# Low part of every second half weight block: ScalarE and an accumulating GpSimd DMA in place of a VectorE subtraction

## The chip, the core and the metric

The kernel runs on one core of a Trainium2 chip. The metric is device time in microseconds from launch to end, the median of several executions. The engines named here are TensorE (PE in the profile, PEld for its weight loads), VectorE (DVE), ScalarE (ACT), GpSimd (POOL) and SyncE (SP, which only issues DMAs).

## What is computed

The reference is a two-layer trunk over 256 latent tokens and 256 context tokens of width 2048. Each layer projects all tokens with a 2048 x 8192 weight matrix, runs a gated short convolution on one half of the features and an eight-head bidirectional retention on the other, and projects back with a 2048 x 2048 matrix.

```python
shift, scale, gate = split(silu(c) @ w_mod + b_mod, 3)
hx = rmsnorm(x, norm_w) * (1 + scale) + shift
a_h, a_b, a_c, a_z, q, k, v, r_z = split(hx @ w_in)
y_conv = silu(a_z) * rmsnorm(a_b * short_conv(a_c * a_h, conv_w), conv_norm_w)
y_ret  = silu(r_z) * headnorm(retention(rope(q), rope(k), v, states of the context))
x = x + gate * (concat(y_conv, y_ret) @ w_out)
```

The context goes through the same layer in layer 0. In layer 1 only its keys and values are needed, since the output holds the 256 latent tokens alone. After the second layer there is a last RMSNorm.

## The kernel before

**Precision.** All large products are made of float32 numbers split in two parts of TensorE's reduced type (fp32r): a high part, which is the rounded number, and a low part, which is the number minus its high part. `split` (L368) makes both: ScalarE writes the high part (L369), VectorE subtracts (L370). `mm3` (L343) then adds three products: high by high, high by low, low by high. Where only the 256 latent tokens are needed, `mmx` (L350) has the same three products in two matmuls per block, one of 512 columns (L353) for the high weights and one of 256 columns (L354) for the low weights.

**Weights.** Weights come in *pieces* of 128 x 1024 float32 numbers (512 KB, eight blocks of 128 x 128), in the order in which TensorE uses them. SyncE loads a piece into one of `RAW` = 6 buffers named `raw`. There are 512 pieces: 256 of `w_in` (`wi`), 64 of `w_out` (`wo`), 64 (`wm`) and 128 (`wd`) of the modulation matrix. Only the first two kinds are split, by *half pieces* of 128 x 512 numbers (four blocks), into the tiles `whi` and `wlo`. Both have `WH` = 4 buffers, so a half piece takes the buffers that the half piece four places before it has left. `pump` (L287) issues loads and splits in program order as buffers come free; it is called after each half piece that TensorE has been given (`block_done`, L335), so every engine's order is fixed when the program is written.

```python
WH, AHEAD = 4, 3
if self.wsplit - self.wused >= self.WH or s > self.at + self.AHEAD: break
self.split(self.raw[s][:, 512 * hf:512 * hf + 512], hi, lo)
```

A `raw` buffer is given to a new load once the instructions that read its second half have ended.

**Order.** `build_program` (L197) lists the steps. Per layer: first the seven tiles of `P` (all rows of weights, seven output tiles at once), then one tile of 128 output features after the other (`F`: conv tiles A_*, then per head K, Q and R_Z), with two steps `V` for the values, then `OG` and `O` for the output projection. In layer 1 the K tiles and V run over 512 tokens (`mm3`); conv tiles, Q, R_Z and the output projection run over 256 (`mmx`). Steps `D` between them are rows of the modulation matrix, which VectorE multiplies and sums (L535). A `P`, `F` or `O` tile of 16 blocks uses two pieces, that is four half pieces.

In layer 1, pieces over 256 tokens are 64 for the conv tiles (with `P`), 16 for Q, 16 for R_Z and 32 for the output projection.

Of the kernel before, what the change touches and what calls it, by code (L numbers as in the profile page):

```python
# [13 lines left out]
AF = mybir.ActivationFunctionType  # L14
ALU = mybir.AluOpType
# [5 lines left out]
NX = 256  # L21
# [3 lines left out]
EPS = 1e-6  # L25
# [140 lines left out]
class Trunk:  # L166
# [25 lines left out]
    def bank(self, kind, name="b"):  # L192
        return self.psum.tile([P, NT], F32, tag=kind, name=name)

# [1 line left out]

    def build_program(self):  # L197
        prog = []
# [88 lines left out]
    def pump(self):  # L287
        nc = self.nc
        while True:
            did = False  # L290
            while self.nload < len(self.seq) and (self.nload < self.RAW or self.free[self.nload - self.RAW]):
                kind, i = self.seq[self.nload]
                t = self.praw.tile([P, 1024], F32, tag="raw", name="raw")
                nc.sync.dma_start(t, self.io[kind][i])
                self.raw[self.nload] = t
                self.nload += 1
                did = True
            while self.nsplit < 2 * self.nload:
                s, hf = divmod(self.nsplit, 2)
                if self.weight(s):  # L300
                    if self.wsplit - self.wused >= self.WH or s > self.at + self.AHEAD:
                        break
                    hi = self.pw.tile([P, 512], F32R, tag="whi", name="whi")
                    lo = self.pw.tile([P, 512], F32R, tag="wlo", name="wlo")
                    self.split(self.raw[s][:, 512 * hf:512 * hf + 512], hi, lo)
                    self.parts[s, hf] = (hi, lo)
                    self.wsplit += 1
                    if hf == 1:
                        self.free[s] = True
                        del self.raw[s]  # L310
                elif s > self.at + self.AHEAD:
                    break
                self.nsplit += 1
                did = True
            if not did:
                return
# [21 lines left out]
            del self.parts[s, b // 4]  # L338
            self.pump()

# [1 line left out]

    def mm3(self, out, w, h, first, last):  # L343
        (whi, wlo), (hhi, hlo) = w, h
# [3 lines left out]
        mm(out, lhsT=wlo, rhs=hhi, start=False, stop=last)  # L348

    def mmx(self, out, w, t, first, last):  # L350
        """As mm3, for the NX tokens of t alone; the two halves of out have to be added."""
        mm = self.nc.tensor.matmul
        mm(out.rearrange("p (s t) -> p s t", s=2), lhsT=w[0], rhs=t[:, :, :NX], start=first, stop=False)  # L353
        mm(out[:, :NX], lhsT=w[1], rhs=t[:, 0, :NX], start=False, stop=last)  # L354
# [7 lines left out]
    def mm(self, out, w, t, n, first, last):  # L362
        if n == NX:
            self.mmx(out, w, t, first, last)
        else:
            self.mm3(out, w, (t[:, 0, :], t[:, 1, :]), first, last)

    def split(self, src, hi, lo):  # L368
        self.nc.scalar.activation(hi, src, AF.Copy)  # L369
        self.nc.vector.tensor_tensor(lo, src, hi.bitcast(F32), op=ALU.subtract)  # L370

    def smv(self, name):
        lo, hi = SM[name]
        return self.sm[:, lo:hi]
# [52 lines left out]
        nc.vector.tensor_scalar(self.lg[:, 64:96], e, -256.0, None, op0=ALU.mult)  # L427

    def rsqrt(self, ps, n, dim, out):
        """out = -2 * dim / sqrt(ps / dim + EPS)"""  # L430
        nc = self.nc
        r, t = self.tmp("rr")[:, :n], self.tmp("rt")[:, :n]
        nc.scalar.activation(r, ps, AF.Abs_reciprocal_sqrt, scale=1.0 / dim, bias=self.eps)
        nc.scalar.activation(t, r, AF.Square)
        nc.vector.scalar_tensor_tensor(t, ps, dim * EPS, t, op0=ALU.add, op1=ALU.mult)
        nc.vector.scalar_tensor_tensor(out, t, -3.0 * dim, r, op0=ALU.add, op1=ALU.mult)
# [43 lines left out]
        self.nc.tensor.matmul(ps, lhsT=self.ones, rhs=src, start=True, stop=True)  # L480
        self.rsqrt(ps, n, dim, out)

# [1 line left out]

    def mod_step(self, idx):
        nc = self.nc
# [64 lines left out]
            self.h[k] = self.pair("h")  # L551
        self.split(xn, self.h[k][:, 0, cols], self.h[k][:, 1, cols])

# [1 line left out]

    def n_tok(self, l, f):
        return NT if l == 0 or K <= f < R_Z else NX
# [75 lines left out]
        self.split(src, y[:, 0, :], y[:, 1, :])  # L633
        self.y[k] = y

# [1 line left out]

    def conv_post(self, l, j, pc, ph, pb, pz):
        nc = self.nc
# [30 lines left out]
        nc.vector.scalar_tensor_tensor(sz[:, :n], sz[:, :n], 1.0, pz[:, :n], op0=ALU.add, op1=ALU.mult)  # L670
        return sz

# [1 line left out]

    def rope(self, ps, n):
        nc = self.nc
# [30 lines left out]
        return t1, t2  # L707

    def attend(self, l, h, st):
        """The steps of one head's retention, each with work for TensorE."""  # L710
        nc = self.nc
        n = NT if l == 0 else NX
        q, k, v = st["q"], st["k"], st["v"]
        t1, t2 = st["mask"]
        msl = [slice(P, P + NX), slice(0, NX)]
        e = slice(P * (h % 4), P * (h % 4) + P)
        fin = lambda out, ps, m: nc.vector.scalar_tensor_tensor(out, ps, K_SCALE, m, op0=ALU.mult, op1=ALU.mult)
        tiles = {}

        def parts(name, w):  # L720
            s = self.tmp(name)[:, :w]
            hi, lo = self.tmp(name + "h", dt=F32R)[:, :w], self.tmp(name + "l", dt=F32R)[:, :w]
            return s, hi, lo

        def score(out, c, qc):
            self.mm3(out, (k[0][:, c], k[1][:, c]), (q[0][:, qc], q[1][:, qc]), True, True)

        def ctx_scores(t):
            ps = self.bank("att", "sc")[:, :n]
            score(ps, slice(NX + P * t, NX + P * t + P), slice(0, n))  # L730
            s, hi, lo = parts("sc", n)
            fin(s[:, :NX], ps[:, :NX], t2[:, msl[t]])
            if l == 0:
                fin(s[:, NX:], ps[:, NX:], t1[:, msl[t]])
            self.split(s, hi, lo)
            tiles[t] = (hi, lo)

        def x_scores():
            ps = self.bank("att", "sx")
            s, hi, lo = parts("sx", NT)  # L740
            for t in range(2):
                c = slice(NX * t, NX * t + NX)
                score(ps[:, c], slice(P * t, P * t + P), slice(0, NX))
                fin(s[:, c], ps[:, c], t1[:, msl[t]])
            self.split(s, hi, lo)
            tiles[2] = (hi, lo)

        def weigh(t):
            if t == 0:
                st["po"] = self.bank("att", "po")  # L750
            po = st["po"]
            hi, lo = tiles[t]
            if t < 2:
                self.mm3(po[:, :n], (v[0][:, 2 + t, e], v[1][:, 2 + t, e]), (hi, lo), t == 0, False)
                return
            for i in range(2):
                c = slice(NX * i, NX * i + NX)
                self.mm3(po[:, :NX], (v[0][:, i, e], v[1][:, i, e]), (hi[:, c], lo[:, c]), False, i == 1)
            sq = self.tmp("osq")[:, :n]
            nc.scalar.activation(sq, po[:, :n], AF.Square)  # L760
            hi, lo = self.tmp("osh", dt=F32R)[:, :n], self.tmp("osl", dt=F32R)[:, :n]
            self.split(sq, hi, lo)
            st["sq"] = (hi, lo)

        def finish():
            ps = self.bank("att", "st")[:, :n]
            for i in range(2):
                nc.tensor.matmul(ps, lhsT=self.onesr, rhs=st["sq"][i], start=(i == 0), stop=(i == 1))
            r = self.tmp("hr")[:, :n]
            self.rsqrt(ps, n, P, r)  # L770
            g = self.slot("yf") if l == 0 else self.tmp("yg")
            nc.vector.scalar_tensor_tensor(g[:, :n], st["po"][:, :n], self.smc("gn", l * 8 + h), r,
                                           op0=ALU.mult, op1=ALU.mult)
            nc.vector.tensor_tensor(g[:, :n], g[:, :n], st["sz"][:, :n], op=ALU.mult)
            self.yf[8 + h] = g
            if l == 1:
                self.y_prep(l, 8 + h)

        def run(*fns):
            return lambda: [f() for f in fns]  # L780

        return [run(lambda: ctx_scores(0), lambda: ctx_scores(1)), run(lambda: weigh(0), x_scores),
                lambda: weigh(1), lambda: weigh(2), finish]

# [1 line left out]

    def load_res(self, l, f):
        if f >= KT:
# [29 lines left out]
        elif segs[0] == 0:  # L818
            nc.scalar.dma_start(self.scratch[f], o[:, :NX])

# [1 line left out]

    def run(self):
        nc = self.nc
# [171 lines left out]
```

## Time and profile before

| | before |
|---|---|
| time, median of 2 runs | 1576.28 us (1575.01 to 1577.54) |
| span of the profiled execution | 1574.7 us |
| TensorE busy | 1537.8 us, 98% |
| VectorE busy | 1153.4 us, 73% |
| ScalarE busy | 701.5 us, 45% |
| GpSimd busy | 0.7 us, 0% |
| mean granted TensorE clock | 0.995 of full speed |
| bytes moved by DMAs | 287.24 MB, mean 182 GB/s |

The span runs from the first to the last instruction of one profiled execution. The times of the two runs are 0.3 and 2.8 us above it. A matmul that the profile shows as 0.40 us long overlaps the next; what a matmul costs is the distance from one start to the next.

### The profile page before, as it was taken

What the parts mean: (1) busy time and instruction counts of PE and PEld (TensorE: products, weight loads), DVE (VectorE), ACT (ScalarE), POOL (GpSimd) and SP (SyncE); (2) the same over time, 40 slices, a digit from 0 to 9 for tenths busy, and PEclk for the clock granted to TensorE, in tenths of its full rate; (3) what the DMA queues carried; (4) which work ended last, traced back from release to release, by engine and by line L of the source; (5) the groups of instructions that cost most, each with busy time, mean ns of one, the idle gap of its engine ahead of it and who ended that gap; (6) DMA issues with size and microseconds to landing.
All of it is one profiled execution on the core that took longest, in us unless ns stands there. A gap on an engine that the chain in (4) does not pass through costs nothing.

```text
span 1574.7 us, 20880 instructions
## 1 busy us (share of the span) xinstructions
PE 1537.8 (98%) x7486; PEld 1249.8 (79%) x7486; DVE 1153.4 (73%) x2236; ACT 701.5 (45%) x1243; POOL 0.7 (0%) x6
## 2 busy tenths in 40 slices
PE   4999999999999999999999999999999999999996
PEld 2556888888888888888888888888888888888885
DVE  4345997777767666776678887889886877677775
ACT  4223432222224444344545332566553565466663
POOL 0000000000000000000000000000000000000000
PEclk9999999999999999999999999999999999999998
DMA  8989575555653233433335776556786444443563
GB/s 316 341 294 328 181 223 190 184 181 192 195 172 121 94 114 105 158 119 99 116 95 176 248 229 211 154 183 216 264 284 201 133 126 139 164 148 108 174 217 104
DMA packets 84631, 287.24 MB, mean 182 GB/s; under 512 B 9392, under 2 KB 13616, under 8 KB 84400
## 3 DMA queue, kind: packets, MB, share of 16 engines
q1 hardware_dynamic: 81648, 282.77, 54.9%
q10 hardware_dynamic: 2880, 3.15, 0.6%
q8 instruction: 58, 0.95, 0.2%
q14 instruction: 45, 0.37, 0.1%
HBM read 281.69 MB, written 4.19 MB: 182 GB/s over the span
## 4 chain that ended last, share of the span: by engine, by line
PE 95%; DVE 2%; ACT 1%; DMA 1%; issue 0%; SPq 0%; DVEq 0%; ACTq 0%
PE acc L346 16%; PE acc L348 16%; PE acc L347 16%; PE acc L353 12%; PE acc L354 6%; PE vps L348 4%; PE vps L347 4%; PE vps L346 4%; PE mod L496 2%; PE p L346 2%; PE p L347 2%; PE p L353 2%; PE p L348 2%; PE ops L353 1%; PE ops L346 1%; PE ops L347 1%
## 5 line engine op out<-in xcount | busy, mean ns | idle before, releaser
L369 ACT ACTIVATE whi<-raw 128x512 fp32r<-128x512 f32 x640 | 402.1, 631 | 662.4 <-PE acc L347 353.7
L370 DVE TENSOR_TENSOR wlo<-raw,whi 128x512 fp32r<-128x512 f32 x640 | 437.4, 688 | 235.8 <-ACT whi L369 220.2
L346 PE MATMUL acc<-h,whi 128*128 128x512 f32 x912 | 355.7, 390 | 1.6 <-DVE vc L603 1.6
L348 PE MATMUL acc<-h,wlo 128*128 128x512 f32 x912 | 355.3, 390 | 0.0
L347 PE MATMUL acc<-h,whi 128*128 128x512 f32 x912 | 355.2, 389 | 0.0
L353 PE MATMUL acc<-h,whi 128*128 128x512 f32 x656 | 232.7, 398 | 0.0
L346 PEld LDWEIGHTS acc<-h,whi 128*128 128x128 f32 x912 | 171.2, 188 | 37.2 <-ACT whi L369 2.4
L348 PEld LDWEIGHTS acc<-h,wlo 128*128 128x128 f32 x912 | 171.2, 188 | 35.8
L347 PEld LDWEIGHTS acc<-h,whi 128*128 128x128 f32 x912 | 171.2, 188 | 34.7
L354 PE MATMUL acc<-h,wlo 128*128 128x256 f32 x656 | 184.3, 281 | 0.0
L353 PEld LDWEIGHTS acc<-h,whi 128*128 128x128 f32 x656 | 123.2, 188 | 29.7
L535 DVE CUSTOM_DVE_ANT_0 junk<-raw,cb,sm 128x1024 bf16<-128x1024 f32 x112 | 142.1, 1278 | 0.1
L535 DVE CUSTOM_DVE_ANT_0 junk<-raw,cb,mvp 128x1024 bf16<-128x1024 f32 x112 | 141.8, 1278 | 0.1
L354 PEld LDWEIGHTS acc<-h,wlo 128*128 128x128 f32 x656 | 123.9, 189 | 0.2
L346 PE MATMUL vps<-whi,h 128*128 128x512 f32 x256 | 100.4, 392 | 0.0
L348 PE MATMUL vps<-whi,h 128*128 128x512 f32 x256 | 99.8, 390 | 0.0
L347 PE MATMUL vps<-wlo,h 128*128 128x512 f32 x256 | 99.7, 390 | 0.0
L347 PE MATMUL acc<-y,whi 128*128 128x512 f32 (+1 forms) x208 | 77.7, 374 | 0.0
L348 PE MATMUL acc<-y,wlo 128*128 128x512 f32 (+1 forms) x208 | 77.5, 373 | 0.0
L346 PE MATMUL acc<-y,whi 128*128 128x512 f32 (+1 forms) x208 | 77.5, 373 | 0.0
L353 PE MATMUL acc<-y,whi 128*128 128x512 f32 x192 | 67.9, 399 | 0.0
L346 PEld LDWEIGHTS vps<-whi,h 128*128 128x128 f32 x256 | 48.1, 188 | 10.1 <-issue 0.2
(194 smaller groups left out, 1977.7 us busy)
## 6 DMA issues: line engine op xcount, KB each, us to landing
raw<-wi SPq DMA_DIRECT2D x256, 512.0 KB, 3.8
raw<-wd SPq DMA_DIRECT2D x128, 512.0 KB, 4.3
raw<-wm SPq DMA_DIRECT2D x64, 512.0 KB, 6.0
raw<-wo SPq DMA_DIRECT2D x64, 512.0 KB, 3.7
xs<-xc SPq DMA_DIRECT2D x16, 256.0 KB, 5.4
xr<-xc SPq DMA_DIRECT2D x16, 256.0 KB, 5.5
cb<-cb SPq DMA_DIRECT2D x1, 2048.0 KB, 11.1
scratch<-x ACTq DMA_DIRECT2D x16, 128.0 KB, 3.7
```

What stands on the lines that cost most here:

```text
L346: mm(out, lhsT=whi, rhs=hhi, start=first, stop=False)
L347: mm(out, lhsT=whi, rhs=hlo, start=False, stop=False)
L348: mm(out, lhsT=wlo, rhs=hhi, start=False, stop=last)
L353: mm(out.rearrange("p (s t) -> p s t", s=2), lhsT=w[0], rhs=t[:, :, :NX], start=first, stop=False)
L354: mm(out[:, :NX], lhsT=w[1], rhs=t[:, 0, :NX], start=False, stop=last)
L369: self.nc.scalar.activation(hi, src, AF.Copy)
L370: self.nc.vector.tensor_tensor(lo, src, hi.bitcast(F32), op=ALU.subtract)
L496: nc.tensor.matmul(self.modps[32 * j:32 * j + 32, :n], lhsT=self.csp[:, k, :], rhs=raws[o // 1024][:, o % 1024:o % 1024 + n], start=(i == ...
L535: nc.vector.tensor_tensor_reduce(junk, raw, self.cb[:, D * m + 1024 * hf:D * m + 1024 * hf + 1024], 1.0, init, ALU.mult, ALU.add, out[:, f ...
```

## The change

In the pieces from number 256 on, the low part of the second half piece is no longer made by VectorE. ScalarE writes the high part as before, then writes the negated raw block into `wlo` (it is rounded to fp32r there in the same way as the high part), and GpSimd issues a DMA that adds the raw block to `wlo` in place. 198 of the 256 last pieces are weights that are split; all others of the 640 half pieces keep the old way. Piece 256 is the first of the last K tile of layer 0, so the change covers that head's three tiles, layer 0's output projection and all of layer 1.

```diff
+                    src = self.raw[s][:, 512 * hf:512 * hf + 512]
+                    if hf == 1 and s >= 256:
+                        self.split_dma(src, hi, lo)
+                    else:
+                        self.split(src, hi, lo)
-                    self.split(self.raw[s][:, 512 * hf:512 * hf + 512], hi, lo)
...
+    def split_dma(self, src, hi, lo):
+        nc = self.nc
+        nc.scalar.activation(hi, src, AF.Copy)
+        nc.scalar.activation(lo, src, AF.Copy, scale=-1.0)
+        nc.gpsimd.dma_start(lo, src, accum_op=ALU.add)
```

The rows below are the program's order of one engine, with the source line, the operation, and output and input tiles with their buffer names. First ScalarE before, in layer 1's output projection, around one output tile (two pieces, four half pieces):

```order
L369 ACTIVATE whi_14249<-raw_14084 128x512
L455 ACTIVATE sq_14234<-x2_14231 128x256
L817 ACTIVATE x2_14231<-x2_14231,sm_84 128x256
L369 ACTIVATE whi_14261<-raw_14084 128x512
L369 ACTIVATE whi_14273<-raw_14110 128x512
L369 ACTIVATE whi_14285<-raw_14110 128x512
```

ScalarE after, at the same place; `sq` and `x2` belong to the previous output tile:

```order
L466 ACTIVATE sq_14428<-x2_14425 128x256
L373 ACTIVATE whi_14443<-raw_14273 128x512
L828 ACTIVATE x2_14425<-x2_14425,sm_84 128x256
L379 ACTIVATE whi_14455<-raw_14273 128x512
L380 ACTIVATE wlo_14456<-raw_14273 128x512
L373 ACTIVATE whi_14468<-raw_14300 128x512
L379 ACTIVATE whi_14480<-raw_14300 128x512
L380 ACTIVATE wlo_14481<-raw_14300 128x512
```

One more instruction stands behind the high part of each second half piece. VectorE before, at the same place:

```order
L808 SCALAR_TENSOR_TENSOR x2_14231<-acc_14182,mv1_141,xr_14057 128x256
L370 TENSOR_TENSOR wlo_14228<-raw_14049,whi_14227 128x512
L811 SCALAR_TENSOR_TENSOR x2_14231<-acc_14182,mv1_141,x2_14231 128x256
L370 TENSOR_TENSOR wlo_14250<-raw_14084,whi_14249 128x512
L456 TENSOR_TENSOR ssq_13660<-ssq_13660,sq_14234 128x256
L370 TENSOR_TENSOR wlo_14262<-raw_14084,whi_14261 128x512
L370 TENSOR_TENSOR wlo_14274<-raw_14110,whi_14273 128x512
```

VectorE after:

```order
L819 SCALAR_TENSOR_TENSOR x2_14425<-acc_14374,mv1_141,xr_14245 128x256
L822 SCALAR_TENSOR_TENSOR x2_14425<-acc_14374,mv1_141,x2_14425 128x256
L467 TENSOR_TENSOR ssq_13836<-ssq_13836,sq_14428 128x256
L374 TENSOR_TENSOR wlo_14444<-raw_14273,whi_14443 128x512
L374 TENSOR_TENSOR wlo_14469<-raw_14300,whi_14468 128x512
```

Every second subtraction is gone from VectorE. Each of them is a DMA on GpSimd's queue now, which had none before:

```order
L381 DMA wlo_14396<-raw_14210 128x512
L381 DMA wlo_14421<-raw_14237 128x512
L381 DMA wlo_14456<-raw_14273 128x512
L381 DMA wlo_14481<-raw_14300 128x512
L381 DMA wlo_14513<-raw_14337 128x512
```

These are five of the 198; nothing else stands between them on that queue.

## Rows read from the trace of the kernel before

**Rows 1.** Page, part 1: busy us, share of the span, instructions.

```profile
span 1574.7 us, 20880 instructions
...
PE 1537.8 (98%) x7486; PEld 1249.8 (79%) x7486; DVE 1153.4 (73%) x2236; ACT 701.5 (45%) x1243; POOL 0.7 (0%) x6
```

**Rows 2.** Page, part 4: share of the ending chain by engine.

```profile
PE 95%; DVE 2%; ACT 1%; DMA 1%; issue 0%; SPq 0%; DVEq 0%; ACTq 0%
```

**Rows 3.** Busy time by stretch (us from the span's start).

```profile
core 0: us, PE busy (x) PEld busy (x) DVE busy (x) ACT busy (x) POOL busy (x), PEclk, DMA share, GB/s
20.00:40.00 20.00, 16.67 (x108) 8.42 (x108) 7.85 (x22) 4.50 (x8) 0.00 (x0) 0.83 0.81 309
970.00:1180.00 210.00, 209.87 (x1197) 182.69 (x1196) 177.54 (x380) 119.92 (x236) 0.00 (x0) 1.00 0.67 218
1100.00:1165.00 65.00, 65.00 (x371) 56.33 (x370) 54.82 (x106) 35.19 (x67) 0.00 (x0) 1.00 0.82 274
1180.00:1450.00 270.00, 269.00 (x1352) 225.38 (x1351) 200.23 (x414) 146.96 (x275) 0.00 (x0) 1.00 0.46 147
1450.00:1555.00 105.00, 104.97 (x600) 90.83 (x599) 77.33 (x149) 66.36 (x124) 0.00 (x0) 1.00 0.54 171
```

**Rows 4.** Page, part 5: the two halves of the weight split.

```profile
L369 ACT ACTIVATE whi<-raw 128x512 fp32r<-128x512 f32 x640 | 402.1, 631 | 662.4 <-PE acc L347 353.7
L370 DVE TENSOR_TENSOR wlo<-raw,whi 128x512 fp32r<-128x512 f32 x640 | 437.4, 688 | 235.8 <-ACT whi L369 220.2
```

**Rows 5.** ScalarE's groups by line, 970 to 1165 us.

```profile
L369 ACT ACTIVATE whi<-raw 128x512 fp32r<-128x512 f32 x129 | 81.3, 632 | 70.9 <-PE acc L353 42.0 <-PE p L353 11.2 <-PE acc L347 10.4
```

**Rows 6.** Timeline of ScalarE, layer 1's output projection: start us, us.

```profile
1497.69 0.63 ACT L369 ACTIVATE whi<-raw 128x512 fp32r<-128x512 f32 x1
1498.23 0.49 ACT L817 ACTIVATE x<-x,sm 128x256 f32<-128x256 f32 x1
1499.10 0.63 ACT L369 ACTIVATE whi<-raw 128x512 fp32r<-128x512 f32 x1 [0.38 <-PE acc L353]
```

**Rows 7.** Timeline of TensorE over the same weights.

```profile
1498.90 0.28 PE L354 MATMUL acc<-y,wlo 128*128 128x256 f32 x1
...
1502.08 0.28 PE L354 MATMUL acc<-y,wlo 128*128 128x256 f32 x1
...
1503.49 0.28 PE L354 MATMUL acc<-y,wlo 128*128 128x256 f32 x1
```

**Rows 8.** DMA view, whole span: KB each, median us to landing.

```profile
xr<-xc SPq DMA_DIRECT2D x16, 256.0 KB, 5.5
...
out<-fo SPq DMA_DIRECT2D x4, 256.0 KB, 2.3
```

**Rows 9.** DMA view, 970 to 1165 us.

```profile
q1 hardware_dynamic: 11168, 40.66, 64.7%
...
raw<-wi SPq DMA_DIRECT2D x62, 512.0 KB, 4.2
raw<-wd SPq DMA_DIRECT2D x16, 512.0 KB, 4.4
scratch<-x ACTq DMA_DIRECT2D x3, 128.0 KB, 1.7
```

**Rows 10.** View of the tile raw, same stretch, its last row.

```profile
DMA to landing us min/median/max: 3.3/4.3/7.5
```

**Rows 11.** Tile xr: its issue on SyncE's queue, ns min/median/max.

```profile
L792 SPq DMA_DIRECT2D xr<-xc x16: 383/424/433, 841.9 to 958.2; - x16
```

**Rows 12.** Timeline of TensorE near the start: idle time in brackets.

```profile
27.80 0.80 PE L346 MATMUL p<-h,whi 128*128 128x512 f32 x1 [1.31 <-ACT whi L369]
28.39 0.63 PE L347 MATMUL p<-h,whi 128*128 128x512 f32 x1
28.82 0.63 PE L346 MATMUL p<-h,whi 128*128 128x512 f32 x1
```

## The prediction

> **What bounds the kernel now.** I read the page's busy times and its chain first: TensorE is busy for 98% of the span and carries 95% of the chain that ended last [rows 1, 2]. VectorE, from which the change takes work, carries 2%. So VectorE is not what the time waits for as a whole. Then the busy times by stretch, for layer 1, which holds most of the changed half pieces: from 970 to 1555 us TensorE is busy for 209.87 + 269.00 + 104.97 = 583.84 of 585 us [rows 3]. All that a faster VectorE could give back there is 1.2 us, although VectorE itself is nearly as full (177.54 of 210 us in the conv tiles). What matters is therefore whether each low part is still there in time.
>
> How early it is made is read from the timelines of ScalarE and TensorE in layer 1's output projection. The high part of one second half piece starts at 1499.10 us, when TensorE gives up the buffer: its last matmul with the old low part starts at 1498.90 and lasts 0.28 [rows 6, 7]. TensorE reads the new low part first at 1503.49. So **4.39 us** lie between. That is no accident of this place: four buffers leave three half pieces of work for TensorE between a buffer's release and its next use, and one half piece over 256 tokens takes 1503.49 - 1502.08 = 1.41 us [rows 7]. In the conv stretch the grouped waits say the same: most of what ScalarE waits for ahead of a high part is TensorE, 42.0 of 70.9 us from one line alone [rows 5]; it starts as soon as a buffer is released and not before. The old way needs 0.63 us for the high part and 0.69 us for the subtraction [rows 4], 1.3 us of the 4.39.
>
> **The change part by part.** *Removed:* 198 subtractions of 688 ns [rows 4], 136 us of VectorE. By the first paragraph this is worth 0 to 1.2 us; I take 1.
>
> *Added on ScalarE:* 198 copies at 631 ns [rows 4], 125 us. In the conv tiles 64 of them bring ScalarE from 119.92 to 160 of 210 us, in the output projection 32 bring it from 66.36 to 87 of 105 [rows 3]: more, but with room. The new copy waits for TensorE's last use of the old low part; that ended at 1499.18, before the copy can start. What is queued behind it (the next high part, then `sq` and the scaling of `x2`) moves by one copy, about 0.6 us, and those high parts have some 3 us to spare. Nothing here.
>
> *Added in the chain of each changed low part:* copies follow each other by 0.54 us (1497.69 to 1498.23) and last 0.63 [rows 6], so the negated block is ready 1.17 us after the high part starts. Then comes X, the time from there until GpSimd's DMA has landed. TensorE waits if 1.17 + X is over 4.39, that is **if X is over 3.2 us**. It waits at the first matmul that reads the low part and everything behind it in its order waits too. The chain restarts at the release four half pieces earlier, and within it lies one other changed half piece, whose stall counts for both; so each changed half piece costs half of the excess, (1.17 + X - 4.39) / 2.
>
> *How many pay:* of layer 1's pieces over 256 tokens, 64 for the conv tiles, 16 for R_Z and 32 for the output projection, 112 in all with the short window. The 16 of Q have a K tile (twice the work) or a head's own matmuls ahead of them; I put 4 us for them all, an estimate. K, V and layer 0 run over 512 tokens, where three half pieces are about twice 4.2 us; they pay only if X is over some 7 us.
>
> *What X is.* No row shows a DMA that GpSimd issues or one that adds. Bounds from other DMAs: below, 2.3 us for a 256 KB store in the quiet end of the kernel [rows 8], and even 1.7 us for 128 KB in the conv stretch [rows 9]; above, 7.5 us, the slowest landing of a raw piece in that stretch [rows 10]. Nothing lands in less than the lower ones, so a negative cost has no ground beyond VectorE's 1 us. Between them, an adding DMA has to read its source and its destination, 512 KB for a 256 KB block, and it does so beside the weight loads, whose own queue already fills 64.7% of the 16 engines [rows 9] and 82% with all traffic in 1100 to 1165 us [rows 3]. The nearest row by bytes and by load is thus the raw piece, 512 KB in 4.2 to 4.4 us [rows 9, 10]. The 256 KB load in 2 KB rows, the same shape as the block, took 5.5 us [rows 8]. The issue itself took 0.42 us for such a shape on SyncE's queue [rows 11], and GpSimd has to issue too, so I add it in full: X = 4.3 + 0.4 = **4.7 us**.
>
> The Trainium skill prices this lower. In DMA: Bandwidth & Descriptors, section "Anatomy of one DMA — SWDGE (gpsimd) path", a DMA issued by GpSimd costs about 2.0 us plus its bytes over 436 GB/s. For 256 KB that is an estimate of 2.6 us, under the point of 3.2, and by it the change would cost nothing. By the same fit the raw pieces would land after 3.2 us: the trace's fastest in the conv stretch, 3.3 us, agrees, its median of 4.3 us does not [rows 10]. No run here shows such a DMA yet.
>
> *Moved or later:* a raw buffer is freed when the DMA has read it, not when VectorE has, so 1.17 + 4.7 - 1.3 = 4.6 us later. Its next load takes 4.3 us. Six buffers cover 6 x 2.8 = 17 us of TensorE's work, 11 us where one piece in three is a modulation row; 8.9 us fit in both. SyncE issues in order, so a residual load behind a waiting weight load comes later as well, but it is used three output tiles on. This cover is gone if X is above 7.
>
> *Sum:* 112 x (5.87 - 4.39) / 2 = 83 us, plus 4 for Q, minus 1 for VectorE: +86 us. The profiled span is 1574.7 us and the median of the runs 1576.3, 1.6 above it; on the median this gives **1662 us**. It is steep: one microsecond of X is 56 us of time.
>
> **The rivals.** *The transfer stays hidden* (not slower). X is at most 3.2 us: the DMA's reads are spread well and it isn't held up by loads. For it speaks the 2.3 us store of the same size [rows 8]; against it the stretch's 4.3 us landings, the second read and the busy engines. It ends at 1575 to 1576 us. The 2% that a measurement of this kernel can tell from no change, 31.5 us, is reached at X = 3.8, so this rival decides between 3.2 and 3.8. The fit of the Trainium skill named above would have this outcome.
>
> *The DMA is much slower* (issue by software, small packets, or adding slows the engines; 198 x 256 KB of reads and writes on engines that are 64.7% to 82% busy hold up the loads too). X is 6 to 7.5 us. Then 112 x (7.17 - 4.39) / 2 = 156, with 16 x 1 us for Q 172, up to 112 x 2.14 = 240 with 16 x 2 for Q 272: 1748 to 1848 us. The 5.5 us row speaks for it, and that the weight loads come every 2.8 us; against it, that TensorE's own stalls thin the loads out.
>
> *The clock falls as well.* Near the start, after TensorE had sat idle for 1.31 us at a time, equal matmuls of 512 columns come 0.43 us apart (28.39, 28.82), the lower level of 1.2 GHz, and the stretch's granted clock is 0.83 [rows 3, 12]. A stall of 0.74 us in each 3.6 us could do the same. If it costs a tenth of the clock over the 112 pieces' 112 x 2.82 = 316 us, that adds 35 us: 1697 us. Against it: at the lower clock the window doubles and the stalls vanish, so it would right itself.
>
> *The gain of VectorE decides.* With TensorE idle for 1.2 us in layer 1 this cannot reach 2%.
>
> **How the numbers follow.** Forecast, X of 3.8 to 6, about 1608 to 1748 us: 0.50. Hidden, within 2%: 0.24. Much slower DMA: 0.20. Lower clock: 0.05. Faster by over 2%: 0.01. So slower 0.75, same 0.24, faster 0.01. The range takes in the hidden case from below, 1574 us, and reaches to X = 6.9 above (112 x 1.84 + 16 x 1 = 222), 1798 us; what lies outside I hold for 0.15.
>
> **What would show it right or wrong.** Right: in layer 1's conv tiles and output projection, TensorE's weight loads at the low matmul (L354, which is L358 in the changed file) wait for the DMA `wlo<-raw` once in each piece, 0.7 us a time, in sum near 80 us; issue to landing of that DMA near 4.7 us; none of it in K, V or layer 0. Wrong: landings of 3 us or less and no wait; or TensorE waiting for raw loads, a granted clock under 1.00 in layer 1, or waits in the wide stages too, which would mean that X is over 7 us.

## The result

The changed kernel takes 1742.74 us (1742.64 to 1742.84), 1.1066 times the kernel before, with an interval of 1.1048 to 1.1083. That is 166 us more.

The profiled execution's first part of the page, against [rows 1]:

```profile
span 1740.9 us, 21523 instructions
...
PE 1591.4 (91%) x7486; PEld 1279.6 (74%) x7486; DVE 1039.4 (60%) x2038; ACT 799.4 (46%) x1441; POOL 171.3 (10%) x204
```

The span grew by 1740.9 - 1574.7 = 166.2 us, and the page splits it in two. TensorE's idle time (span less busy) went from 36.9 to 149.5 us, 112.6 more. Its busy time went from 1537.8 to 1591.4 us, 53.6 more, for the same 7486 matmuls. VectorE has 114 us less to do, and nothing of that shows in the time.

The chain that ended last, by engine and by line, against [rows 2]:

```profile
PE 50%; DMA 24%; issue 21%; DVE 2%; ACT 1%; POOL 1%; SPq 0%; POOLq 0%; ACTq 0%; DVEq 0%
DMA wlo<-raw 22%; PE acc L352 11%; PE acc L350 11%; PE acc L351 11%; PE vps L351 2%; PE vps L350 2%; PE vps L352 2%; PE mod L507 2%; PE p L350 2%; PE p L351 2%; PE p L352 1%; DMA raw<-wo 1%; POOL wlo L381 1%; PE ops L352 1%; PE ops L350 1%
```

TensorE falls from 95% to 50% of it. The adding DMA alone is 22%. Most of the 21% under issue lies between one DMA instruction of GpSimd and the next, where the chain loses what GpSimd waited for (ScalarE's copy, by the timeline); so these are not shares of the time lost. The groups by line tell which matmuls wait and which are longer (busy us, mean ns; then idle time before them):

```profile
L381 POOL DMA_DIRECT2D wlo<-raw x198 | 170.6, 862 | 1551.6 <-ACT wlo L380 1380.9
L358 PE MATMUL acc<-h,wlo 128*128 128x256 f32 x656 | 199.1, 304 | 68.7 <-DMA wlo<-raw 68.5
L357 PE MATMUL acc<-h,whi 128*128 128x512 f32 x656 | 255.0, 424 | 0.0
```

The low matmul of the 256-token tiles (L358) has 68.7 us of idle time before it, all but 0.2 of it ended by the adding DMA. Both kinds of matmul also take longer on the average, 304 and 424 ns against 281 and 398 before:

```profile
L353 PE MATMUL acc<-h,whi 128*128 128x512 f32 x656 | 232.7, 398 | 0.0
...
L354 PE MATMUL acc<-h,wlo 128*128 128x256 f32 x656 | 184.3, 281 | 0.0
```

This is the clock for the most part: a high matmul (L357) took 610 ns in the mean where the granted clock was at its lower level (1.2 GHz) and 397 elsewhere. The stretches of layer 1 (TensorE busy in the first column after the length, granted clock and DMA share behind POOL), against [rows 3], where the clock was 1.00 throughout layer 1:

```profile
core 0: us, PE busy (x) PEld busy (x) DVE busy (x) ACT busy (x) POOL busy (x), PEclk, DMA share, GB/s
980.00:1060.00 80.00, 66.95 (x373) 57.35 (x372) 36.88 (x87) 42.96 (x88) 15.61 (x18) 0.96 0.77 189
1060.00:1180.00 120.00, 91.23 (x441) 75.91 (x441) 59.94 (x142) 62.95 (x128) 24.11 (x28) 0.90 0.80 200
1180.00:1290.00 110.00, 86.70 (x393) 71.62 (x392) 45.19 (x87) 48.98 (x93) 19.77 (x23) 0.88 0.85 228
1350.00:1590.00 240.00, 226.80 (x1142) 188.33 (x1142) 132.10 (x286) 153.66 (x291) 41.88 (x49) 0.99 0.72 178
1590.00:1720.00 130.00, 103.45 (x523) 86.20 (x523) 50.27 (x99) 73.98 (x140) 26.92 (x32) 0.92 0.79 193
```

The conv tiles (1060 to 1290 us) and the output projection (1590 to 1720) have lost both busy time and clock; the heads between them, mostly 512-token tiles, much less. The row of the page with the clock in 40 slices shows the same two places:

```profile
PEclk9999999999999999999999999988899999999898
```

Not all of the 53.6 us of longer busy time is the clock. The mean granted clock was 0.970 of full speed against 0.995, so the clock took at most 0.030 x 1740.9 - 0.005 x 1574.7 = 44 us. Compared matmul by matmul with the trace of before, 38 us of the longer busy time lie where the clock was at its lower level (some 85 us of time between 1020 and 1700 us, in short spells). The other 15 us lie beside waits: there a matmul counts as busy for its full 0.39 or 0.40 us, while in an unbroken row only its distance to the next counts. So TensorE waited 113 + 15 = 128 us more, and the clock cost about 38 us.

What one wait looks like, in the timeline of layer 1's output projection, against [rows 6, 7]; TensorE's idle time stands in brackets:

```profile
1638.14 0.63 ACT L379 ACTIVATE whi<-raw 128x512 fp32r<-128x512 f32 x1 [0.53 <-PE acc L357]
...
1638.68 0.62 ACT L380 ACTIVATE wlo<-raw 128x512 fp32r<-128x512 f32 x1
...
1639.59 0.86 POOL L381 DMA_DIRECT2D wlo<-raw  x1 [2.08 <-ACT wlo L380]
...
1642.74 0.39 PE L358 MATMUL acc<-y,wlo 128*128 128x256 f32 x1 [2.87 <-DMA wlo<-raw]
```

The high part starts when its buffer is released, the negated block follows 0.54 us later and ends at 1639.30, GpSimd starts at 1639.59 and TensorE's low matmul can start at 1642.74. From the end of ScalarE's work to TensorE's start there are 3.44 us, of which TensorE waited for 2.87. Over all 198, the view of the tile (ns of GpSimd's instruction; then issue to landing):

```profile
L381 POOL DMA_DIRECT2D wlo<-raw x198: 859/859/1010, 771.8 to 1722.7; - x198
...
DMA to landing us min/median/max: 3.2/4.2/8.2
```

And the waits (us in total, times, longest):

```profile
PEld acc L358 <- DMA wlo<-raw: 102.8, 50, 4.6
...
ACT whi L373 <- DMA raw<-wo: 55.4, 13, 7.2
...
ACT whi L373 <- DMA raw<-wi: 40.0, 18, 5.1
```

TensorE's weight loads at L358 waited 102.8 us in 50 waits, about two us each. ScalarE waited 95 us for raw pieces where it had waited 26 us for `wi` before.

### The profile page after: what moved, and what is told of

Read it like the earlier page. It is cut to its first block, busy times and chain, and to the rows that moved or that the text cites. A ratio compares the mean times of both kernels' runs of the same rounds, so it can differ in the third digit from the quotient of the medians.

```text
span 1740.9 us, 21523 instructions
## 1 busy us (share of the span) xinstructions
PE 1591.4 (91%) x7486; PEld 1279.6 (74%) x7486; DVE 1039.4 (60%) x2038; ACT 799.4 (46%) x1441; POOL 171.3 (10%) x204
## 3 DMA queue, kind: packets, MB, share of 16 engines
q0 software_dynamic: 28512, 51.92, 17.2%
## 4 chain that ended last, share of the span: by engine, by line
PE 50%; DMA 24%; issue 21%; DVE 2%; ACT 1%; POOL 1%; SPq 0%; POOLq 0%; ACTq 0%; DVEq 0%
DMA wlo<-raw 22%; PE acc L352 11%; PE acc L350 11%; PE acc L351 11%; PE vps L351 2%; PE vps L350 2%; PE vps L352 2%; PE mod L507 2%; PE p L350 2%; PE p L351 2%; PE p L352 1%; DMA raw<-wo 1%; POOL wlo L381 1%; PE ops L352 1%; PE ops L350 1%
## 5 line engine op out<-in xcount | busy, mean ns | idle before, releaser
L374 DVE TENSOR_TENSOR wlo<-raw,whi 128x512 fp32r<-128x512 f32 x442 | 303.0, 690 | 359.3 <-ACT whi L373 337.5
L350 PE MATMUL acc<-h,whi 128*128 128x512 f32 x912 | 356.0, 390 | 1.1 <-DVE vc L614 1.1
L351 PE MATMUL acc<-h,whi 128*128 128x512 f32 x912 | 355.4, 390 | 0.0
L381 POOL DMA_DIRECT2D wlo<-raw x198 | 170.6, 862 | 1551.6 <-ACT wlo L380 1380.9
L358 PE MATMUL acc<-h,wlo 128*128 128x256 f32 x656 | 199.1, 304 | 68.7 <-DMA wlo<-raw 68.5
L357 PE MATMUL acc<-h,whi 128*128 128x512 f32 x656 | 255.0, 424 | 0.0
L352 PEld LDWEIGHTS acc<-h,wlo 128*128 128x128 f32 x912 | 171.3, 188 | 37.4 <-DMA wlo<-raw 1.4
L350 PEld LDWEIGHTS acc<-h,whi 128*128 128x128 f32 x912 | 171.5, 188 | 36.4 <-ACT whi L373 1.2
L351 PEld LDWEIGHTS acc<-h,whi 128*128 128x128 f32 x912 | 171.5, 188 | 35.0
L358 PEld LDWEIGHTS acc<-h,wlo 128*128 128x128 f32 x656 | 135.3, 206 | 80.7 <-DMA wlo<-raw 80.5
L357 PEld LDWEIGHTS acc<-h,whi 128*128 128x128 f32 x656 | 134.8, 206 | 30.7
L380 ACT ACTIVATE wlo<-raw 128x512 fp32r<-128x512 f32 x198 | 122.1, 617 | 21.4 <-PE vps L351 21.3
L351 PE MATMUL acc<-y,whi 128*128 128x512 f32 (+1 forms) x208 | 77.7, 374 | 0.0
```

What stands on the lines that cost most here:

```text
L350: mm(out, lhsT=whi, rhs=hhi, start=first, stop=False)
L351: mm(out, lhsT=whi, rhs=hlo, start=False, stop=False)
L380: nc.scalar.activation(lo, src, AF.Copy, scale=-1.0)
L381: nc.gpsimd.dma_start(lo, src, accum_op=ALU.add)
```

## The experiments

Each ran beside the kernel before on the same chip; those medians were 1572 to 1574 us, against 1576 us beside the changed kernel. So up to 4 us of a difference between two runs below can be the chip's.

**Without the DMA.**

```diff
         nc.scalar.activation(lo, src, AF.Copy, scale=-1.0)
-        nc.gpsimd.dma_start(lo, src, accum_op=ALU.add)
```

> Leaves out the adding DMA, so the low part of a changed half piece is only the negated block; ScalarE's second copy and VectorE's missing subtractions stay. Theory (the wait is the DMA's latency, 1.17 us of ScalarE plus some 4.7 us against a window of 4.39): nothing waits any more, 1575 us within 5, granted clock 0.995. Rival (the longer order on ScalarE, or its wait for the old low part, delays the high parts): most of the 166 us stays, over 1650 us.

Measured: 1570.54 us, ratio 0.9986 (0.9971 to 1.0).

```profile
span 1568.8 us, 20884 instructions
...
PE 1532.5 (98%) x7486; PEld 1249.0 (80%) x7486; DVE 1037.0 (66%) x2038; ACT 797.2 (51%) x1441; POOL 0.7 (0%) x6
```

All 166 us are the DMA's. ScalarE's second copy costs nothing although ScalarE is busy for 797 us, and taking 198 subtractions from VectorE is worth at most 0.3%. The rival fell.

**The DMA without the add.**

```diff
-        nc.gpsimd.dma_start(lo, src, accum_op=ALU.add)
+        nc.gpsimd.dma_start(lo, src)
```

> The same DMA from GpSimd without the add: it overwrites the low part with the raw block, so it reads 256 KB in place of 512 KB; the order and the waits are the same. Theory (reading the destination and adding is what makes X long): X falls from a median of 4.5 us to about 3.4 us, time about 1600 to 1630 us. Rival (software issue of 0.86 us and the completion of any DMA beside the weight loads make X): X stays at 4.0 us or more, time 1690 to 1740 us.

Measured: 1677.38 us, ratio 1.0672 (1.0631 to 1.0712), between the two forecasts.

```profile
L381 POOL DMA_DIRECT2D wlo<-raw x198: 527/530/670, 773.4 to 1659.3; - x198
...
DMA to landing us min/median/max: 2.2/3.5/6.7
```

GpSimd's instruction is 0.33 us shorter and the fastest landing 1.0 us earlier, 2.2 in place of 3.2 us. The queues (q0 is GpSimd's; last number: share of 16 engines' span), of this run and then of the changed kernel:

```profile
q1 hardware_dynamic: 81648, 282.77, 52.2%
q0 software_dynamic: 28512, 51.92, 9.9%
```

```profile
q1 hardware_dynamic: 81648, 282.77, 49.6%
q0 software_dynamic: 28512, 51.92, 17.2%
```

For the same packets and bytes the adding DMAs hold the engines for 17.2% of 1740.9 us, 1.51 us each; the plain ones for 9.9% of 1677.0, 0.84 us each. So adding lengthens X and loads the engines. It is 65 of the 166 us; some 100 are there for a plain DMA too.

**Every second DMA only.**

```diff
-                    if hf == 1 and s >= 256:
+                    if hf == 1 and s >= 256 and self.wsplit % 4 == 3:
```

> Only every second of the 198 half pieces goes by DMA, one of the four buffers in place of two. Theory (each turn of the four buffers pays the excess of 1.17 + X over 4.39 us once, however many changed half pieces lie in it): nearly all of the cost stays, 1690 to 1740 us, a little less because X shortens with less traffic. Rival (each DMA costs its own share, 166 us over 198): 1650 to 1665 us.

Measured: 1650.03 us, ratio 1.0498 (1.0463 to 1.0532): 78 of 166 us stay, the rival's number.

```profile
DMA to landing us min/median/max: 3.2/3.6/6.9
```

The median landing fell from 4.2 to 3.6 us. To tell the two reasons apart the timeline of the kernel before was replayed: each changed half piece's first low read was put no earlier than its high part's start plus the chain (high part, copy, DMA) measured for that DMA, and the start moved with the release four half pieces before. With every chain at its stage's mean in the changed kernel, all 198 give 95 us of waiting and every second one still 91, so with equal chains a turn of the buffers pays once, as the theory has it. But the chains are not equal. As they were measured in the changed kernel, all 198 give 130 us and every second one 94: of the two in a turn the longer one pays, and with half of them gone so are half of the long ones. With the shorter chains of this run the replay gives 62 us; the trace has 60, counted as in the section on the result. So what halving the number saved in waits comes about half from fewer DMAs and half from a shorter X. Neither forecast had the spread.

**High matmuls first.**

```diff
...
+            for j, w in enumerate(ws):
...
+                mm(out.rearrange("p (s t) -> p s t", s=2), lhsT=w[0], rhs=src[k][:, :, :NX], start=k == 0, stop=False)
+            for j, w in enumerate(ws):
...
+                mm(out[:, :NX], lhsT=w[1], rhs=src[k][:, 0, :NX], start=False, stop=k == 15)
...
```

> In output tiles over 256 tokens the four high matmuls of a half piece come ahead of its four low ones, so the first low read is 3 x 0.23 = 0.69 us later with the buffers released at the same time: window 5.08 in place of 4.39 us. Theory (latency against window): each turn of four buffers saves 0.69 us, some 53 turns, so 37 us less waiting and fewer spells of lower clock: 1670 to 1700 us. Rival (DMA engines or raw loads set the pace): no gain, 1730 us or more.

Measured: 1726.99 us, ratio 1.0987 (1.0937 to 1.1038), 16 us less than the changed kernel and not the 43 to 73 expected.

```profile
DMA to landing us min/median/max: 3.2/4.7/8.3
```

The landings became longer as the window did, 4.7 us in the median for 4.2. A fixed X, which the forecast had assumed, is refuted; what lengthened it is not shown here.

**Five buffers.**

```diff
-    RAW, WH, AHEAD, TMP = 6, 4, 3, 9
+    RAW, WH, AHEAD, TMP = 5, 5, 3, 9
```

> The changed kernel with five buffers for the high and low parts in place of four; SBUF is full, so the raw pieces have five in place of six. Theory (latency against the window of the buffers): the window grows by one half piece, from 4.39 to 5.80 us, against a chain of some 6 us; most of the waiting goes and the clock with it recovers: 1590 to 1630 us. Rival (the DMA engines or the loads set the pace): over 1690 us, and with one raw buffer less still longer.

Measured: 1726.14 us, ratio 1.0976 (1.0938 to 1.1014). The forecast fell.

> Control: the kernel before with the same five and five buffers. TensorE already had no waits worth naming, so 1570 to 1590 us; anything above is what the missing raw buffer costs.

Measured for this control: 1582.09 us, ratio 1.0047 (1.0029 to 1.0064). In the changed kernel with five buffers the waits for raw pieces are:

```profile
ACT whi L373 <- DMA raw<-wi: 189.1, 65, 5.7
ACT whi L373 <- DMA raw<-wo: 93.8, 21, 9.2
```

That is 283 us on ScalarE against 95 with six raw buffers; the control has 199 us of such waits (126.3 for `wi`, 72.9 for `wo`) and is only 8 us longer than the kernel before, so their sum says little. By the low matmuls' times in the two traces of the changed kernel, the short-window stages became shorter (P by 9 us, conv 21, R_Z 10, output projection 10), but layer 0's output projection and V lost 21 and 11 us, which they did not in the control. A raw buffer is freed only when the DMA has read it, and with one buffer less that is no longer hidden. The landings became longer here too:

```profile
DMA to landing us min/median/max: 3.2/4.8/9.0
```

So the run says that the window helps, but not how much it would by itself; SBUF has no room for both.

**Matmuls laid into the waits.**

```diff
+            if n == NX and kk == 4:
...
+                mm(full, lhsT=w[0], rhs=src[k][:, :, :NX], start=False, stop=False)
+                for _ in range(DUMMY):
+                    mm(full[:64], lhsT=self.zero, rhs=src[k][:, :, :NX], start=False, stop=False)
+                mm(out[:, :NX], lhsT=w[1], rhs=src[k][:, 0, :NX], start=False, stop=False)
...
```

`DUMMY` is 3.

> The changed kernel with three matmuls of 512 columns with zero weights (they add nothing) ahead of the first low matmul of the second half piece, in the 106 places of output tiles over 256 tokens in layer 1: 0.69 us of work each, laid where TensorE waits. Theory (54 of the 166 us are matmuls at the lower clock, which falls because TensorE sits idle): the work runs inside the waits, the granted clock rises from 0.97 to about 0.99, 1690 to 1720 us although 73 us of work are added. Rival (the clock has another cause, or the waits are not idle time that can be filled): 1743 to 1816 us.

Measured: 1758.19 us, ratio 1.118 (1.1128 to 1.1232), clock 0.984.

> Control: the same filler in the kernel before, where nothing waits at these places: 106 x 0.69 = 73 us more, 1640 to 1655 us, clock 0.995.

Measured for the control: 1644.72 us, ratio 1.0458 (1.0422 to 1.0494), as expected. Busy times of the changed kernel with filler, and of the control:

```profile
span 1754.1 us, 22149 instructions
...
PE 1640.0 (93%) x7804; PEld 1303.0 (74%) x7804; DVE 1038.5 (59%) x2038; ACT 798.5 (46%) x1442; POOL 171.4 (10%) x204
```

```profile
span 1642.9 us, 21522 instructions
...
PE 1606.1 (98%) x7804; PEld 1290.7 (79%) x7804; DVE 1157.9 (70%) x2236; ACT 706.0 (43%) x1244; POOL 0.7 (0%) x6
```

The filler is 1606.1 - 1537.8 = 68.3 us of busy time. In the changed kernel TensorE's idle time fell by 149.5 - 114.1 = 35.4 us, so half of the filler fitted into waits. The longer busy time fell from 53.6 to 1640.0 - 1606.1 = 33.9 us, and of it the part at the lower clock from 38 to 20 us, which sets right the 54 us of the forecast. The forecast of 1690 to 1720 failed. The waits come unevenly: of the 130 changed half pieces over 256 tokens 75 had none in the changed kernel and 9 had one of 3 us or more, and equal fillers miss them. But less idle time did bring a higher clock for the same DMAs: the two go together.

**Load on the engines without a dependence.**

```diff
                 nc.sync.dma_start(t, self.io[kind][i])
+                if self.nload >= 256 and kind in ("wi", "wo"):
+                    nc.gpsimd.dma_start(self.side[self.nload - 256], t[:, :896])
```

> The kernel before, with VectorE's subtractions, and beside it a plain DMA from GpSimd for each of the last 198 weight pieces, which copies 448 KB of the raw block to a side buffer in HBM that nothing reads. A plain 256 KB DMA took 0.84 us of the 16 engines (9.9% of 1677 us over 198), so 448 KB should take about 1.5 us, as an adding one did (17.2% of 1741 us over 198); a raw piece takes 1.69 us (54.9% of 1575 us over 512). Theory (the engines' time is a bound of its own: conv tiles of layer 1 need 66 x 1.69 + 50 x 1.5 = 187 us for 141 us of TensorE's work): although no low part waits for a DMA here, the loads come late and 40 to 75 us are added, 1615 to 1650 us. Rival (only the latency of the chain to the low part counts): no low part hangs on these DMAs, 1570 to 1585 us.

Measured: 1597.08 us, ratio 1.0153 (1.0125 to 1.0181), nearer to the rival than to the theory.

```profile
q0 software_dynamic: 15840, 90.85, 14.2%
```

```profile
970.00:1200.00 230.00, 217.16 (x1193) 182.77 (x1191) 172.77 (x373) 114.75 (x230) 36.93 (x68) 0.99 0.93 329
```

The side DMAs held the engines for 14.2% of 1598.1 us, 1.15 us each and not 1.5, and the engines were busy for 93% from 970 to 1200 us; TensorE lost 13 of 230 us there. So engines this full cost about 24 us when only the loads hang on them. That price includes raw buffers that came free late: 53 of the side DMAs landed after their piece had been split, 29 of them among the 64 of the conv tiles. Most of the 166 us needs the short chain to the low part as well.

**Half the bytes loaded.**

```diff
-                nc.sync.dma_start(t, self.io[kind][i])
+                if self.nload >= 256 and kind in ("wi", "wo"):
+                    nc.sync.dma_start(t[:, 512:], self.io[kind][i][:, 512:])
+                else:
+                    nc.sync.dma_start(t, self.io[kind][i])
...
+                    if s >= 256:
+                        src = self.raw[s][:, 512:]
```

> The changed kernel, but of the weight pieces from number 256 on only the second half is loaded, 256 KB in place of 512, and both halves are split from it: first half pieces get wrong numbers, instructions stay the same. Theory (load on the DMA engines makes X long and sets the pace): conv tiles now need some 144 us of engine time for 141 of TensorE's work, X falls towards 3.6 us, 1600 to 1640 us. Rival (X is a fixed latency of software DMAs that add): X stays over 4.3 us, 1690 us or more.

Measured: 1677.99 us, ratio 1.0667 (1.0636 to 1.0698).

```profile
DMA to landing us min/median/max: 3.2/3.8/7.7
```

65 us less, by 0.4 us of the median landing. The weight loads are a part of X, but the forecast of 1600 to 1640 fell: the median did not come down to 3.6, and an adding DMA takes 3.2 us at its fastest, which already puts the chain (1.15 + 0.29 + 3.2 = 4.6 us) above the window of 4.39.

**Wide tiles only.**

```diff
-                    if hf == 1 and s >= 256:
+                    if hf == 1 and s >= 256 and s in self.wide:
```

`wide` holds the pieces whose output tile runs over 512 tokens.

> The change only where a tile runs over 512 tokens: layer 0's end, K and V of layer 1, 70 of the 198 DMAs. Three half pieces of work are 8.2 us there. Theory (a chain of 6 us fits, and VectorE is not the bound): no wait, 1568 to 1578 us, within 0.5% of the kernel before. Rival (each DMA costs its share, 166 us over 198): 1630 us.

Measured: 1581.17 us, ratio 1.0057 (1.004 to 1.0073).

```profile
span 1577.9 us, 21144 instructions
...
PE 1535.2 (97%) x7486; PEld 1248.8 (79%) x7486; DVE 1109.7 (70%) x2166; ACT 735.6 (47%) x1313; POOL 61.2 (4%) x76
```

The 70 DMAs with a window of 8 us cost next to nothing, 8 us in place of the rival's 59. The small loss lies in layer 0's output projection and in V. TensorE waited some 6 us for the adding DMA there, and ScalarE waited 57 us for raw pieces of `wo`; which of the two was the first cause is not told apart. The forecast of no wait at all was a little too good.

**High first and half the bytes.** The two edits above together.

> Two earlier edits together: high matmuls first within a half piece (alone 16 us less than the changed kernel), and half the bytes per weight piece from number 256 on (alone 65 us less; first half pieces get wrong numbers). Theory (a longer window lets TensorE run faster, which loads the DMA engines more and lengthens X again; with the loads halved that feedback is weak, so the window pays): the chain from the release of the low part, 0.63 us and some 4.1 to 4.4, meets a window of about 4.9, most waits vanish, 1590 to 1630 us, clock over 0.99. Rival (the order of the matmuls is worth little in itself): the two savings add, 1655 to 1670 us.

Measured: 1647.48 us, ratio 1.0471 (1.0454 to 1.0489). The savings come to 95 us where they were 16 and 65 alone. So the window is worth 30 us with lighter loads and 16 with full ones, which speaks for the feedback but doesn't show it, and the forecast of 1590 to 1630 fell. In the conv tiles the mean of X rose again, from 4.56 us (half the bytes alone) to 5.26, with the bytes unchanged. What lengthens it there stays open; the modulation rows are loaded in full among these tiles in both runs.

## Why the prediction was right in direction and short in size

*VectorE is not the bound.* Right. Without the DMA the kernel is 0.14% faster in the median, 1.65 us (at most 0.3% by the interval); up to 1.2 us was allowed for.

*ScalarE's copies cost nothing; the chain starts 1.17 us late.* Right: ScalarE's part measured 1.15 us in the median, GpSimd started 0.29 us after it. (In 16 half pieces over 512 tokens, in V and just after it, ScalarE's order came out the other way, with the negated block ahead of the high part; little hangs on them.)

*Window of 4.39 us, half of the excess for each changed half piece.* Right. The replay by this rule with the measured chains gives 130, 84, 62 and 88 us of waiting for the changed kernel, the plain, the halved and the half-loaded one; the idle time added in the four traces is 113, 77, 54 and 75. With the matmuls beside waits, counted as in the section on the result, TensorE waited 128, 87, 60 and 90 us more. The rule comes within 4% of all four.

*X = 4.7 us.* Close in the middle, mis-sized as a single number. From the end of ScalarE's copy to the landing the median of the 198 was 4.5 us and the mean 4.8; in the conv tiles the mean was 5.1. With every chain at its stage's mean the replay gives 95 us, near the 86 of the sum; with the real spread 130. A late landing is paid, and an early one is not refunded. This is the first term that was too small: 128 us of waiting for 86. It shows in the signs as well: in place of 0.7 us once in each piece there were 55 waits among the 130 changed half pieces over 256 tokens, of 1.9 us each.

*What X consists of.* The nearest row, a raw piece's 4.3 us, was a lucky guide. An adding DMA landed 3.2 us after its issue at the fastest, 1.0 us later than the fastest plain one; the rest goes with the traffic. In the changed kernel the ten DMAs with no weight load in flight landed after 3.4 us in the mean. With one load in flight at the issue it was 4.0 us (81 DMAs), with two 4.9 (65), with three 6.0 (13). For the plain DMA it was 2.4 us without a load, and 3.2, 4.3 and 5.0 with one, two and three. These were worked out from issue and landing of each DMA in the traces.

*The Trainium skill's fit* of 2.0 us plus bytes over 436 GB/s (DMA: Bandwidth & Descriptors, section "Anatomy of one DMA — SWDGE (gpsimd) path"), an estimate of 2.6 us, agrees with the plain DMA on quiet engines, 2.2 to 2.4 us after the issue and 0.29 us ahead of it. The section gives the fit for DMAs that GpSimd issues; the raw pieces, to which the prediction applied it as well, are issued by SyncE. The fit doesn't cover the add or the traffic, and the measurement decides: the chain doesn't fit, and the rival of a hidden transfer was wrong.

*The clock.* It stood as a rival of its own, with 35 us and a chance of 0.05, and was no part of the sum. It happened along with the stalls, with a granted clock of 0.88 to 0.96 in the conv tiles, which the prediction had named as a sign of being wrong, and cost about 38 us. So its price was right, and what failed was to put it beside the stalls and not on top of them. The reason against it, that the window doubles at 1.2 GHz and the stalls vanish, was no protection, as the clock fell in short spells and each cost its part. With 86 us of the sum, 42 us more of waiting and 38 of the clock the 166 us are complete.

*The range.* The time lies in it, in part by luck: its upper part stood for a mean X of up to 6.9 us, and X was 4.8. The spread and the clock filled that room.

*Raw pieces freed later are covered.* In the main right; ScalarE's waits for them grew from 26 to 95 us, and at most 9 us of that reached TensorE: layer 0's output projection became 5 us longer and V 4, and a part of that is waits for the adding DMA itself. With one raw buffer less these two stages cost 32 us more.

No version beat the kernel before beyond noise. The run without the DMA bounds what taking these 198 subtractions from VectorE can give here: at most 0.3%.

## What to carry to other kernels

A transfer that takes the place of an engine's instruction must fit between the release of its buffer and the next use, so read that window from the trace before anything else, and compare it with the slowest landings under load and not with the median. Where TensorE will stall in many small pieces, add the clock to the bill: here it was 38 us on 128 us of waiting. A matmul beside a wait counts as busy for longer, so take the waits from starts and not from the busy time alone. Widening the window or thinning the traffic each helped less than was forecast, and with a wider window the landings became longer; that a faster pace loads the same DMA engines more would explain it, but no run shows that by itself.

## What was not expected of the hardware

An adding DMA of 128 x 512 float32 numbers from GpSimd held the 16 engines for 1.51 us where the plain one took 0.84, and GpSimd's own instruction took 0.86 us for 0.53. Its landing ranged from 3.2 to 8.2 us for one size and shape. TensorE's granted clock fell to 0.88 over 110 us in which it was busy for 79% of the time by the profile, with waits of some 2 us between.
